# Reordering the steps of a mixer stage: each attention pair behind the states of the same quarter

## The chip, the cores and the metric

The kernel runs on one core of a Trainium2 chip. That core has five engines, each of which works through its own instruction queue in order: TensorE (PE, matrix products; its weight loads are listed as PEld), VectorE (DVE), ScalarE (ACT), GpSimd (POOL) and SyncE (SP, which here issues most of the transfers). Semaphores make one queue wait for another. The metric is the device time of one execution in microseconds (us).

## The reference

Two layers work on x, 512 positions of 1024 features, all in float32. In layer 0 one projection gives four parts of 512 features, u, q, k and v. The part u feeds a diagonal state space model of 32 groups, each with 64 complex states; q, k, v feed eight heads of stick-breaking attention. Both results go through one output projection. Layer 1 has a convolution module instead. Each mixer, and each MLP behind it, is followed by a layer norm over `alpha*x + branch(x)`.

```python
h = x @ mix_w_in[i] + mix_b_in[i]
u, q, k, v = jnp.split(h, [S5_WIDTH, S5_WIDTH + SB_WIDTH, S5_WIDTH + 2 * SB_WIDTH], axis=-1)
...
    # s5_mixer
    bu = jnp.einsum('blgp,gnp->blgn', ug, b_bar)
    _, states = lax.associative_scan(combine, (a, bu), axis=1)
    y = jnp.real(jnp.einsum('blgn,gpn->blgp', states, c)).reshape(bsz, seq, S5_WIDTH)
    y = jax.nn.gelu(y + d.astype(f32) * uf).astype(u.dtype)
    h = y @ w_glu + b_glu
    val, gate = jnp.split(h, 2, axis=-1)
    return val * jax.nn.sigmoid(gate)
...
    # stick_breaking_attention, one block of queries
    z = jnp.einsum('bqhd,bkhd->bhqk', q_blk.astype(jnp.float32), kf) * scale
    log_beta = jax.nn.log_sigmoid(z)
    log_keep = jnp.where(strict, jax.nn.log_sigmoid(-z), 0.0)
    after = lax.cumsum(log_keep, axis=3, reverse=True) - log_keep
    weights = jnp.where(strict, jnp.exp(log_beta + after), 0.0)
    return jnp.einsum('bhqk,bkhd->bqhd', weights, vf)
...
mix = jnp.concatenate([s5_out, sb_out], axis=-1) @ mix_w_out[i] + mix_b_out[i]
```

## The kernel before

Activations lie transposed, features on the partitions and the 512 positions along the free axis. To keep float32 accuracy, each large product is made of three: an operand is split into a high and a low half (`split`, lines 196 and 197; for weights lines 86 to 90, where ACT writes `whi` and DVE writes `wlo`), and `gemm` (line 206) adds high x high, high x low and low x high. One 128 x 512 output tile over eight feature tiles thus takes 24 products.

The change touches the mixer stage of layer 0, about the first 275 us. Its steps are:

- u0 to u3: four projections that give u. `u0` is spread between the transposes of x at the very start (line 298), the others come from `in_proj`. Each result is copied out of PSUM by ACT (`ue`), written to DRAM and read back in another layout as `U` (lines 592 and 594).
- the parameters of the state space model: a chain of small DVE operations (`sm`), and the output matrices `Craw`, loaded by SP and transposed by PE (`cp`, line 582) into `Cd`.
- `tables(q)`: sines and cosines for quarter q of the groups, eight scalings and three further passes on ACT and five passes on DVE, into tiles `tc` and `ts`.
- q0 to q3 (`qkv`): for one pair of heads the three projections q, k and v, 72 products. The halves of q and k (`qh`, `ql`, `kh`, `kl`) are made from PSUM by ACT and DVE.
- s0 to s3 (`s5_states`): for a quarter of the groups DVE builds the matrices `Gx` and `Cx`, PE transposes `Gx` (`gp`, line 513), multiplies (`tp` line 521, `vR` line 533, `vI` line 535), and DVE rotates by the tables, scans (lines 549 and 550) and rotates back into `Sx`.
- y0 to y3 (`s5_outputs`): twelve products (`yp`, lines 563 and 565) and the update of `U`.
- a0 to a3 (`attention`): for one pair of heads transposes of v (`vt`), scores (`z`, line 646), the softplus on ACT and DVE (`sp`), a causal select on POOL (line 638), a split (`sh`, `sl`), triangular sums added to the scores (line 670), an Exp (`w`), another select, and the product with v (`av`, line 679).
- gelu (Tanh on ACT, then through DRAM into another layout, `Yd` and `yf`), glu (products `gg` and `gv`, a Sigmoid) and at last the mixer's output product, first its half from glu (`acmo`), then its half from the attentions.

The list `ORDER` is the order in which the steps are emitted. It isn't yet the order on the engines. A planner at build time lets each engine take, among the instructions that it reckons to be ready, the one emitted first; the weight loads and splits of this stage are ranked ahead of all else. Buffers of one tag are handed out in the order of emission. PSUM has three banks under the tag `mm` (projections, `gg`, `gv`, `acmo`), four under the tag `z` (states, scores, `vt`, `yp`, `cp`) and one for `av`. The tables have three buffers each, `qh` and `ql` two each, `kh` and `kl` one each; weights are prepared up to two units ahead into three slots.

ACT holds one set of function tables at a time. `Act` (line 137 loads a set) ties each load behind all functions of the set before in the order of emission, so sets change in that order only: Sin for the tables, Exp and Ln for the attentions, Tanh for gelu, Sigmoid for glu.

Of the kernel before, what the change touches and what calls it, by code (L numbers as in the profile page):

```python
# [9 lines left out]
F32 = mybir.dt.float32  # L10
# [6 lines left out]
P = 128  # L17
T = 512
# [26 lines left out]
ATT = "sB0 sC0 wB0 sA0 wC0 sB1 sC1 wB1 sA1 wC1 wA1 wA0"  # L45
MIX_BUFS = (3, 4, 1, 4, 3)
WARM = 24
QK_BUFS = (2, 1)
ORDER = "q0 s0 q1 y0 t3 s1 a0 y1 s2 q2 y2 s3 a1 y3 gelu a2 q3 glu a3".split()


class Weights:
# [56 lines left out]
def units_of(name, w, k0, nk, cols, width):  # L109

    ncol = 1024 // nk
    out = []
    for c in cols:
        base = c // width * width
        src = w[k0 * P : (k0 + nk) * P, base : base + width].rearrange("(k p) n -> p k n", p=P)
        out.append(((name, k0, base), src, nk, ncol, c - base, width))
    return out
# [29 lines left out]
def kernel(ctx: ExitStack, tc: tile.TileContext, a: dict, out: bass.AP):  # L147
    nc = tc.nc
    act = Act(tc)
    V, S, G, PE = nc.vector, nc.scalar, nc.gpsimd, nc.tensor  # L150
# [4 lines left out]
    def const(shape, name, dt=F32):  # L155
        return cst.tile(shape, dt, tag=name, name=name)
# [5 lines left out]
    ident = const([P, P], "ident")  # L162
# [27 lines left out]
    def pv(n, i):  # L190
        if n == "mix_b_in":
            return PB[:, i : i + 1]
        return PV[:, vrow[n] + i : vrow[n] + i + 1]
# [6 lines left out]
    def gemm(ps, w, ksl, xs, c0, c1, start=True, stop=True):  # L200
        hi, lo = w
        n = len(xs)
        for k in range(n):
            xh, xl = xs[k]
            for i, (u, v) in enumerate(((hi, xh), (hi, xl), (lo, xh))):
                ins = PE.matmul(ps[:, c0:c1], u[:, k, ksl], v[:, c0:c1], start=start and k == 0 and i == 0,  # L206
                                stop=stop and k == n - 1 and i == 2).ins
        return ins
# [6 lines left out]
    s5 = mix.enter_context(tc.tile_pool(name="s5", bufs=1))  # L215

    w_in, w_glu, w_out = a["mix_w_in"][0], a["s5_w_glu"][0], a["mix_w_out"][0]
    units = units_of("u", w_in, 0, 8, range(0, 512, 128), 128)
    for o in ORDER:
        if o[0] == "q":  # L220
# [8 lines left out]
    def psum(tag, name, bufs):  # L229
        return mps.tile([P, T], F32, tag=tag, name=name, bufs=bufs)  # L230

    def mm(name):
        return psum("mm", name, MIX_BUFS[0])

    def zz(name):
        return psum("z", name, MIX_BUFS[1])
# [22 lines left out]
    xin = []  # L259
    with tc.high_priority():  # L260
        for j in range(KT):
            tag, bufs = (("spt", MIX_BUFS[3]), ("wt", MIX_BUFS[4]), ("qh", QK_BUFS[0]))[(0, 1, 0, 1, 0, 1, 0, 2)[j]]
            xt = att.tile([P, 4, P], F32, tag=tag, name=f"xin{j}", bufs=bufs)
            nc.sync.dma_start(xt, a["x"][0][:, P * j : P * (j + 1)].rearrange("(b p) f -> p b f", p=P))
            xin.append(xt)
# [3 lines left out]
    Craw = [s5.tile([P, 4, P], F32, tag="sp", name=f"Craw{i}", bufs=6) for i in range(2)]  # L269
# [22 lines left out]
    xs, w0, u0 = [], None, mm("u0")  # L292

    def u0_part(k, after):

        xh, xl = xs[k]
        for i, (u, v) in enumerate(((w0[0], xh), (w0[0], xl), (w0[1], xh))):
            ins = PE.matmul(u0, u[:, k], v, start=k == 0 and i == 0, stop=k == KT - 1 and i == 2).ins
            tc.add_manual_dep(ins, after, NOSYNC, reason="order of the first products")
            after = ins.name  # L300
        return ins

    u0_last = ready
    for j in range(KT):
        ps = (mm if j % 2 else s5ps)(f"xT{j}")
# [12 lines left out]
        if j > 1:  # L318
            u0_last = u0_part(j - 2, ins.name)
# [9 lines left out]
    for k in (KT - 2, KT - 1):  # L329
        u0_last = u0_part(k, u0_last.name)  # L330
# [10 lines left out]
    def ts(o, x, s1, s2, op0, op1):  # L341
        V.tensor_scalar(o, x, s1, s2, op0=op0, op1=op1)
        return o
# [77 lines left out]
    for k in (2, 3, 4):  # L421
        h = 1 if k < 4 else 2
# [31 lines left out]
    def spage(name, tag="sp", bufs=6):  # L454
        return s5.tile([P, 4, P], F32, tag=tag, name=name, bufs=bufs)

    tabs = []

    def tables(q):
        fa, fb, fr = spage(f"fa{q}"), spage(f"fb{q}"), spage(f"fr{q}")  # L460
        for r in range(4):
            k = 4 * q + r
            act(fa[:, r], cix, AF.Copy, scale=uh[:, k : k + 1])
            act(fb[:, r], cix, AF.Copy, scale=ul[:, k : k + 1])
        ts(fr, fa, MAGIC, MAGIC, ALU.add, ALU.subtract)
        V.tensor_tensor(fa, fa, fr, op=ALU.subtract)
        V.tensor_tensor(fa, fa, fb, op=ALU.add)
        ts(fr, fa, MAGIC, MAGIC, ALU.add, ALU.subtract)
        V.tensor_tensor(fa, fa, fr, op=ALU.subtract)
        tc_, ts_ = spage(f"tc{q}", "tabc", 3), spage(f"ts{q}", "tabs", 3)  # L470
        act(ts_, fa, AF.Sin, scale=TWOPI)
        act(fb, fa, AF.Abs)
        act(tc_, fb, AF.Sin, bias=hpi_c, scale=-TWOPI)
        tabs.append((tc_, ts_))

    for q in range(3):
        tables(q)

    Gx = s5.tile([P, 2, 4, 4, 2, 16], F32, tag="Gx", name="Gx")
# [79 lines left out]
    def s5_outputs(q):  # L559
        yp = s5ps(f"yp{q}")  # L560
        for r in range(4):
            o = yp[:, r * P : (r + 1) * P]
            PE.matmul(o, Tx[:, r], U[:, 4 * q + r], start=True, stop=False)
            for i in range(2):
                PE.matmul(o, Cx[:, i, r, 1:5].rearrange("p t g q -> p (t g q)"), Sx[:, i, r], start=False, stop=i == 1)
        for r in range(4):
            stt(U[:, 4 * q + r], U[:, 4 * q + r], DD[:, 4 * q + r : 4 * q + r + 1], yp[:, r * P : (r + 1) * P], ALU.mult, ALU.add)
        vv.append(U[:, 4 * q : 4 * q + 4])


    def in_proj(tile_i, name):
        w = W.next()
        ps = mm(name)
        gemm(ps, w, slice(0, P), xs, 0, T)
        return ps, pv("mix_b_in", tile_i)

    Cd = s5.tile([P, 2, 16, 16], F32, tag="Cd", name="Cd")
    with tc.issue_after(u0_last):
        for i in range(2):
            cp = zz(f"cp{i}")  # L580
            for b in range(4):
                PE.transpose(cp[:, b * P : (b + 1) * P], Craw[i][:, b, :], ident)
            cv = cp.rearrange("p (r g q) -> p r g q", g=2, q=16)
            for h in range(2):
                hp = slice(h * 64, h * 64 + 64)
                V.tensor_copy(Cd[hp, i], cv[hp, :, h, :])
    Ud = [tc.dram_tile([P, T], F32, name=f"Ud{j}") for j in range(4)]
    for j in range(4):
        ps, b = in_proj(j, f"u{j}") if j else (u0, pv("mix_b_in", 0))
        up = att.tile([P, T], F32, tag="wt", name=f"ue{j}", bufs=MIX_BUFS[4])  # L590
        act(up.rearrange("p (t c) -> p c t", t=4), ps.rearrange("p (c t) -> p c t", t=4), AF.Identity, bias=b)
        nc.sync.dma_start(Ud[j], up)
        for t in range(4):
            nc.sync.dma_start(U[32 * t : 32 * t + 32, 4 * j : 4 * j + 4, :],
                              Ud[j].rearrange("(r f) (t c) -> t f r c", r=4, t=4)[t])
# [6 lines left out]
    def qkv(p):  # L602
        r = []
        for s, n in enumerate("qkv"):
            ps, b = in_proj(4 + 4 * s + p, f"{n}{p}")
            if s == 2:
                t_ = att.tile([P, T], F32, tag=n, name=f"{n}{p}")
                act(t_, ps, AF.Identity, bias=b)
            else:
                b = b if s else bq8[:, p : p + 1]  # L610
                t_ = tuple(att.tile([P, T], F32R, tag=n + x, name=f"{n}{x}{p}", bufs=QK_BUFS[s]) for x in "hl")
                act(t_[0], ps, AF.Identity, bias=b)
                stt(t_[1], ps, b, t_[0].bitcast(F32), ALU.add, ALU.subtract)
            r.append(t_)
        return r
# [111 lines left out]
    hq = {}  # L727
    for o in ORDER:
        if o[0] == "q":
            hq[o[1]] = qkv(int(o[1]))  # L730
        elif o[0] == "a":
            attention(int(o[1]), *hq[o[1]])
        elif o[0] == "t":
            tables(int(o[1]))
        elif o[0] == "s":
            s5_states(int(o[1]))
        elif o[0] == "y":
            s5_outputs(int(o[1]))
        elif o == "gelu":
            gelu()  # L740
        else:
            glu()
# [31 lines left out]
    def stp(name):  # L774
        return sps_.tile([P, T], F32, tag="st", name=name)
# [181 lines left out]
    xs, first = tail_norm_lead(cat[4:8], "a", rb[0], ("ln1_g", 0), ("ln1_b", 0), LEAD, "fl0")  # L957
# [7 lines left out]
    for f in range(2):  # L965
        wn = tmp(f"wn{f}")[:CONV]
        nc.sync.dma_start(wn, a["conv_w_dw"][0][:, f * T : (f + 1) * T])
        ps = stp(f"wd{f}")
# [8 lines left out]
    xs, first = tail_norm_lead(hs, "b", rb[1], ("ln2_g", 0), ("ln2_b", 0), 4, "pl")  # L977
# [58 lines left out]
    cs_, ws, ps = None, [None] * KT, [None] * KT  # L1036
# [16 lines left out]
    for c0, c1 in HALVES:  # L1053
# [9 lines left out]
        r = ln.norm(ys, c0, c1)  # L1063
# [12 lines left out]
    xs, first = tail_norm_lead(cs_, "d", None, ("ln1_g", 8), ("ln1_b", 8), LEAD, "fl1")  # L1076
# [109 lines left out]
```

## Time and profile before

| what | value |
| --- | --- |
| median of 3 runs | 1262.05 us (1260.14 to 1264.09) |
| the profiled execution | 1257.71 us |
| its span | 1255.9 us |
| PE busy | 1203.1 us |
| DVE busy | 777.0 us |
| ACT busy | 565.1 us |
| POOL busy | 111.5 us |
| mean granted clock of PE | 0.984 |

A row of the timeline shows the start, the duration (both in us), the engine, the line, the operation and `out<-in`, then how many instructions it merges; brackets hold the idle time before it and what ended that. A name is that of the tile with buffer numbers left out, so `z1B` is a score tile of attention 1 and `q` stands for all four q projections. A row of stretches gives the length, the busy time of each engine in it with the number of instructions, then the clock that PE was granted (1.00 is full), the share of the transfer engines in use and the GB/s. Products overlap, so a product that shows 0.39 us follows the one before it after some 0.23 us. In a row of waits stand the waiting engine with its tile, who released it, the total in us, the number of waits and the longest.

### The profile page before, as it was taken

What the parts mean: (1) busy time and instruction counts of PE and PEld (TensorE: products, weight loads), DVE (VectorE), ACT (ScalarE), POOL (GpSimd) and SP (SyncE); (2) the same over time, 40 slices, a digit from 0 to 9 for tenths busy, and PEclk for the clock granted to TensorE, in tenths of its full rate; (3) what the DMA queues carried; (4) which work ended last, traced back from release to release, by engine and by line L of the source; (5) the groups of instructions that cost most, each with busy time, mean ns of one, the idle gap of its engine ahead of it and who ended that gap; (6) DMA issues with size and microseconds to landing.
All of it is one profiled execution on the core that took longest, in us unless ns stands there. A gap on an engine that the chain in (4) does not pass through costs nothing.

```text
span 1255.9 us, 16680 instructions
## 1 busy us (share of the span) xinstructions
PE 1203.1 (96%) x6559; PEld 1017.5 (81%) x6559; DVE 777.0 (62%) x1321; ACT 565.1 (45%) x1020; POOL 111.5 (9%) x145
## 2 busy tenths in 40 slices
PE   8999988999999999999999999789899999999997
PEld 6886765778988888888999889679898888888885
DVE  5996953548843433433468999999872442444446
ACT  5755465633622422323345566886462341323230
POOL 1002021103000000000031001123500000000000
PEclk8999998999999999999999999899899999999999
DMA  7520111141432333332223221004052232323211
GB/s 189 162 66 17 52 47 55 51 147 55 146 102 91 99 101 101 101 101 100 73 69 100 68 68 35 1 1 135 1 172 96 68 134 67 105 79 117 85 51 67
DMA packets 111662, 105.93 MB, mean 84 GB/s; under 512 B 9378, under 2 KB 99746, under 8 KB 111584
## 3 DMA queue, kind: packets, MB, share of 16 engines
q1 hardware_dynamic: 111424, 104.84, 26.7%
q8 instruction: 51, 0.84, 0.3%
q14 instruction: 27, 0.22, 0.1%
q10 hardware_dynamic: 160, 0.03, 0.0%
HBM read 100.66 MB, written 4.19 MB: 83 GB/s over the span
## 4 chain that ended last, share of the span: by engine, by line
PE 71%; DVE 15%; issue 6%; ACT 4%; DMA 2%; SPq 1%; POOL 1%; DVEq 0%; POOLq 0%; ACTq 0%
PE f L206 23%; PE g L1116 11%; PE acf L206 10%; PE fl L206 4%; PE h L1100 3%; PE tld L206 3%; DVE cz L350 3%; PE tlb L206 2%; PE cv L1015 2%; DVE wlo L90 2%; DVE cy L350 2%; PE av L679 2%; PE acmo L206 1%; PE pl L206 1%; PE pv L206 1%
## 5 line engine op out<-in xcount | busy, mean ns | idle before, releaser
L89 ACT CAST whi<-raw 128x1024 fp32r<-128x1024 f32 x176 | 183.8, 1049 | 409.4 <-PE f L206 111.3
L90 DVE TENSOR_TENSOR wlo<-raw,whi 128x1024 fp32r<-128x1024 f32 x176 | 219.4, 1250 | 222.9 <-ACT whi L89 222.3
L1116 PE MATMUL g<-whi,hh 128*128 128x512 f32 x208 | 81.5, 392 | 0.0
L1116 PE MATMUL g<-wlo,hh 128*128 128x512 f32 x208 | 81.5, 392 | 0.0
L1116 PE MATMUL g<-whi,hl 128*128 128x512 f32 x208 | 81.4, 391 | 0.0
L206 PE MATMUL f<-xdh,whi 128*128 128x512 f32 x208 | 80.9, 389 | 0.0
L206 PE MATMUL f<-xah,whi 128*128 128x512 f32 x208 | 80.9, 389 | 0.0
L206 PE MATMUL f<-xal,whi 128*128 128x512 f32 x208 | 80.9, 389 | 0.0
L206 PE MATMUL f<-xdh,wlo 128*128 128x512 f32 x208 | 80.9, 389 | 0.0
L206 PE MATMUL f<-xdl,whi 128*128 128x512 f32 x208 | 80.9, 389 | 0.0
L206 PE MATMUL f<-xah,wlo 128*128 128x512 f32 x208 | 80.9, 389 | 0.0
L206 PE MATMUL acf<-hl,whi 128*128 128x512 f32 x192 | 75.2, 392 | 0.0
L206 PE MATMUL acf<-hh,whi 128*128 128x512 f32 x192 | 74.9, 390 | 0.0
L206 PE MATMUL acf<-hh,wlo 128*128 128x512 f32 x192 | 74.7, 389 | 0.0
L196 ACT CAST hh<-fr 128x512 fp32r<-128x512 f32 x64 | 39.7, 621 | 71.4 <-DVE fr L346 71.3
L197 DVE TENSOR_TENSOR hl<-fr,hh 128x512 fp32r<-128x512 f32 x64 | 44.2, 691 | 37.3 <-ACT hh L196 37.2
L350 DVE SCALAR_TENSOR_TENSOR cy<-hp,wdw,cy 128x512 f32<-128x512 f32 (+1 forms) x91 | 60.8, 677 | 0.1
L350 DVE SCALAR_TENSOR_TENSOR cz<-hp,wdw,cz 128x512 f32<-128x512 f32 (+1 forms) x86 | 59.7, 698 | 0.1
L1015 PE MATMUL cv<-hph,dh 128*128 128x256 f32 (+1 forms) x113 | 39.5, 350 | 10.0 <-ACT hph L196 8.3
L346 DVE TENSOR_TENSOR fr<-fr 128x512 f32<-128x512 f32 x64 | 43.7, 684 | 5.4 <-ACT fr L135 5.4
L1116 PEld LDWEIGHTS g<-whi,hl 128*128 128x128 f32 x208 | 39.1, 188 | 8.6
L1116 PEld LDWEIGHTS g<-wlo,hh 128*128 128x128 f32 x208 | 39.1, 188 | 8.6
(684 smaller groups left out, 3182.8 us busy)
## 6 DMA issues: line engine op xcount, KB each, us to landing
raw<-in_ffn_w_dram SPq DMA_DIRECT2D x48, 1024.0 KB, 5.4
raw<-in_ffn_w_dram SPq DMA_DIRECT2D x32, 512.0 KB, 3.4
raw<-in_conv_w_pw_dram SPq DMA_DIRECT2D x12, 1024.0 KB, 5.3
raw<-in_mix_w_in_dram SPq DMA_DIRECT2D x16, 512.0 KB, 3.9
xin<-in_x_dram SPq DMA_DIRECT2D x8, 256.0 KB, 4.1
raw<-in_s_w_glu_dram SPq DMA_DIRECT2D x4, 512.0 KB
raw<-in_mix_w_out_dram SPq DMA_DIRECT2D x4, 512.0 KB
raw<-in_mix_w_out_dram SPq DMA_DIRECT2D x2, 1024.0 KB
```

What stands on the lines that cost most here:

```text
L89: i0 = nc.scalar.copy(hi, raw).ins
L90: i1 = nc.vector.tensor_sub(lo, raw, hi.bitcast(F32)).ins
L196: i0 = S.copy(hi, src).ins
L197: i1 = V.tensor_sub(lo, src, hi.bitcast(F32)).ins
L206: ins = PE.matmul(ps[:, c0:c1], u[:, k, ksl], v[:, c0:c1], start=start and k == 0 and i == 0, stop=stop and k == n - 1 and i == 2).ins
L346: V.tensor_tensor(o, x, y, op=op)
L350: V.scalar_tensor_tensor(o, x, s, y, op0=op0, op1=op1)
L679: PE.matmul(av[R, P * kb :], vt[:, kb, R], w_[:, o : o + T - P * kb], start=summed[h] == 1, stop=summed[h] == 4, skip_group_check=True)
L1015: PE.matmul(cps[j][:, c0:c1], u, v[:, t + c0 : t + c1], start=t == 0 and i == 0, stop=t == n - 1 and i == 2)
L1100: PE.matmul(ps, u, v, start=k == 0 and i == 0, stop=k == nk - 1 and i == 2)
L1116: PE.matmul(pss[b], u, v[:, kk, :], start=k + kk == 0 and i == 0, stop=k + kk == nb - 1 and i == 2)
```

## The change

The emission order becomes s, a, the next projections, y for each quarter: a0 moves from behind s1 to behind s0, a1 from behind s3 to behind s1, a2 from behind gelu to behind s2, and q3 ahead of y2 and s3. Only a3 stands behind gelu, and glu comes last. All four tables are made up front, so `tables(3)` leaves the list (`t3`), and the tables get a fourth buffer each; `qh` and `ql` lose one buffer each. The transposes of `Craw` and the copies into `Cd` are put into a function that is called behind the projection u1, where they stood behind u0. The order of the weight units stays what it was.

```diff
-QK_BUFS = (2, 1)
-ORDER = "q0 s0 q1 y0 t3 s1 a0 y1 s2 q2 y2 s3 a1 y3 gelu a2 q3 glu a3".split()
+QK_BUFS = (1, 1)
+ORDER = "q0 s0 a0 q1 y0 s1 a1 q2 y1 s2 a2 q3 y2 s3 y3 gelu a3 glu".split()
...
-        tc_, ts_ = spage(f"tc{q}", "tabc", 3), spage(f"ts{q}", "tabs", 3)
+        tc_, ts_ = spage(f"tc{q}", "tabc", 4), spage(f"ts{q}", "tabs", 4)
...
-    for q in range(3):
+    for q in range(4):
         tables(q)
...
+    proj_last = []
+    Cd = s5.tile([P, 2, 16, 16], F32, tag="Cd", name="Cd")
+
+    def c_states(last):
+        with tc.issue_after(last):
+            for i in range(2):
+                cp = zz(f"cp{i}")
+                for b in range(4):
+                    PE.transpose(cp[:, b * P : (b + 1) * P], Craw[i][:, b, :], ident)
+                cv = cp.rearrange("p (r g q) -> p r g q", g=2, q=16)
+                for h in range(2):
+                    hp = slice(h * 64, h * 64 + 64)
+                    V.tensor_copy(Cd[hp, i], cv[hp, :, h, :])
+
     def in_proj(tile_i, name):
         w = W.next()
         ps = mm(name)
-        gemm(ps, w, slice(0, P), xs, 0, T)
+        proj_last[:] = [gemm(ps, w, slice(0, P), xs, 0, T)]
         return ps, pv("mix_b_in", tile_i)
 
-    Cd = s5.tile([P, 2, 16, 16], F32, tag="Cd", name="Cd")
-    with tc.issue_after(u0_last):
...
     for j in range(4):
         ps, b = in_proj(j, f"u{j}") if j else (u0, pv("mix_b_in", 0))
+        if j == 1:
+            c_states(proj_last[0])
...
-        elif o[0] == "t":
-            tables(int(o[1]))
```

More of the change, by code (lines that the diff above doesn't have):

```diff
@@ L261 @@
         for j in range(KT):
-            tag, bufs = (("spt", MIX_BUFS[3]), ("wt", MIX_BUFS[4]), ("qh", QK_BUFS[0]))[(0, 1, 0, 1, 0, 1, 0, 2)[j]]
+            tag, bufs = (("spt", MIX_BUFS[3]), ("wt", MIX_BUFS[4]), ("qh", 1))[(0, 1, 0, 1, 0, 1, 0, 2)[j]]
             xt = att.tile([P, 4, P], F32, tag=tag, name=f"xin{j}", bufs=bufs)
@@ L573, in in_proj @@
         ps = mm(name)
-        gemm(ps, w, slice(0, P), xs, 0, T)
+        proj_last[:] = [gemm(ps, w, slice(0, P), xs, 0, T)]
         return ps, pv("mix_b_in", tile_i)
-    Cd = s5.tile([P, 2, 16, 16], F32, tag="Cd", name="Cd")
-    with tc.issue_after(u0_last):
[L579 to L586, printed above, removed]
     Ud = [tc.dram_tile([P, T], F32, name=f"Ud{j}") for j in range(4)]
```

## The prediction

> **What bounds the kernel now.** I read the page first, then the busy times by stretches cut at the steps of the mixer stage (the one stage that the change touches), then what ended the waits there.
>
> ```profile
> span 1255.9 us, 16680 instructions
> PE 1203.1 (96%) x6559; PEld 1017.5 (81%) x6559; DVE 777.0 (62%) x1321; ACT 565.1 (45%) x1020; POOL 111.5 (9%) x145
> PE 71%; DVE 15%; issue 6%; ACT 4%; DMA 2%; SPq 1%; POOL 1%; DVEq 0%; POOLq 0%; ACTq 0%
> ```
> ```profile
> core 0: us, PE busy (x) PEld busy (x) DVE busy (x) ACT busy (x) POOL busy (x), PEclk, DMA share, GB/s
> 16.40:57.20 40.80, 37.03 (x156) 30.10 (x155) 32.61 (x124) 25.30 (x52) 0.64 (x1) 0.92 0.62 161
> 57.20:81.80 24.60, 23.95 (x185) 20.45 (x184) 22.28 (x38) 12.83 (x24) 0.63 (x1) 1.00 0.30 86
> 81.80:119.70 37.90, 34.13 (x237) 25.32 (x236) 27.73 (x51) 21.74 (x43) 6.92 (x13) 1.00 0.10 29
> 119.70:139.90 20.20, 19.46 (x165) 16.28 (x164) 19.45 (x36) 5.53 (x9) 0.82 (x1) 1.00 0.16 53
> 139.90:178.80 38.90, 35.38 (x233) 26.09 (x232) 27.29 (x49) 24.10 (x47) 9.01 (x12) 0.96 0.09 28
> 178.80:221.20 42.40, 37.01 (x154) 25.22 (x153) 20.17 (x34) 27.98 (x51) 3.90 (x12) 0.92 0.22 62
> 221.20:256.90 35.70, 33.61 (x156) 23.47 (x154) 17.22 (x26) 23.45 (x41) 4.11 (x12) 1.00 0.14 45
> 256.90:274.80 17.90, 17.04 (x75) 13.80 (x75) 10.04 (x12) 5.64 (x6) 0.00 (x0) 1.00 0.49 166
> ```
>
> PE is the bound, and its work stays the same: every matrix product is still there. So the change can only move PE's losses: idle time, and clock that the throttle did not grant. In the rows of stretches, loss is length minus PE busy, plus (1 - clock) times PE busy. From 57.2 on that is 0.65 (s0, q1, k1, v1); 3.77 (s1, a0, y1); 0.74 (s2, y2); 3.52 + 1.42 = 4.94 (s3, a1, y3); 5.39 + 2.96 = 8.35 (gelu and a2, the first output gates); 2.09 (a3); 0.86 (first mixer output): 21.4 us. Before 57.2 it is 3.77 + 2.96 = 6.7 us. The whole change plays for these 28 us.
>
> **Part by part.** *The transposes of the output matrices, behind the second unit.* PE now sits before them:
>
> ```profile
> PE cp L582 <- DMA Craw<-in_s_c_im_dram: 2.1, 1, 2.1
> PE cp L582 <- DMA Craw<-in_s_c_re_dram: 1.7, 1, 1.7
> 22.00:27.00 5.00, 5.00 (x15) 3.90 (x13) 2.48 (x18) 0.00 (x0) 0.00 (x0) 0.52 0.11 25
> 29.46 1.05 ACT L89 CAST whi<-raw 128x1024 fp32r<-128x1024 f32 x1 [10.26 <-DMA raw<-in_mix_w_in_dram]
> 30.55 1.23 DVE L90 TENSOR_TENSOR wlo<-raw,whi 128x1024 fp32r<-128x1024 f32 x1 [5.73 <-ACT whi L89]
> 40.75 0.47 PE L206 MATMUL q<-x0h,whi 128*128 128x512 f32 x1
> 41.02 0.39 ACT L135 ACTIVATE fa<-cix,sm 128x128 f32<-128x128 f32 x1
> 45.35 1.18 ACT L135 ACTIVATE ue<-u,PB 128x512 f32<-128x512 f32 x1
> 36.05 0.68 DVE L467 TENSOR_TENSOR fa<-fa,fb 128x512 f32<-128x512 f32 x1
> ```
>
> Those 3.8 us of idle, and 2.4 us (5.00 x 0.48) of the throttled clock behind them, go: unit u1 can run from 16.5 to about 22, by which time the transposes' data is there, and u2 to about 29.3. But u3 is late next: its split weights are ready at 30.5 (high) and 31.8 (low), by the rows of the third load, and these do not move. So PE idles some 2 us there; u3 ends near 37, where q0 now starts at 40.75. Then q0, k0, v0 follow, and these need PSUM that ACT frees: the copy of u3 sits at 45.35, and the fourth sine and cosine table, now emitted with the other three, puts four microseconds of ACT work (8 scalings that start 0.3 us apart though each shows 0.39, and three passes of some 0.6) ahead of it, and some 2.5 us on DVE (five passes of up to 0.68) ahead of s0's matrices. Only 1.4 to 2.9 us of the lead survive to v0's end; I take 2.0. The ends: 0, if the table eats all, and 6.7, the whole loss of the stretch. The table's DVE time is hidden: q1's 24 products (5.5 us) can run while s0 waits. Its old place cost nothing either (PE lost 0.65 us in that stretch).
>
> *Attention behind the same quarter's states.* The "z" banks are handed out in program order, four in all, to states and attention alike; so one states step and the attention behind it form one serial window, filled by projections. The old order has two such windows, s1 with a0 and s3 with a1, 37.9 and 38.9 us long; the new one has four, and the first three have q1 to q3 (72 products each) as filling. Nothing new in them on PE, so each keeps a loss like the two rows: 3.77 and 4.94, mean 4.35, three times 13.05 us. Ends: 2.09 each (the row of a3, where DVE is half idle) and 4.94 plus a starved mask (below).
>
> *The last window.* Filling runs as early as it can (q3 is emitted behind a2, and now starts at 132.44, ahead of s3, a1 and a2), so q3, k3 and v3 are used up in a2's window. From s3's first transpose to the first sigmoid, PE has only s3, y3, a3 and what of the gate products fits in three PSUM banks:
>
> ```profile
> 132.44 0.48 PE L206 MATMUL q<-x0h,whi 128*128 128x512 f32 x1
> 139.87 1.04 PE L513 MATMUL gp<-ident,Gx 128*128 128x128 f32 x8
> 143.16 1.16 PE L533 MATMUL vR<-U,gt 128*128 128x128 f32 x8
> 144.16 1.06 PE L535 MATMUL vI<-U,gt 128*128 128x128 f32 x8
> 146.05 1.72 PE L521 MATMUL tp<-Cx,Gx 128*32 128x128 f32 x62
> 79.10:82.00 2.90, 2.84 (x24) 2.64 (x23) 0.00 (x0) 1.00 0.38 113
> 221.20:256.90 35.70, 18.02 (x72) 12.95 (x71) 1.00 0.14 45
> 145.84 0.69 DVE L346 TENSOR_TENSOR m<-vR,tc 128x512 f32<-128x512 f32 x1
> 154.08 1.27 DVE L346 TENSOR_TENSOR Sx<-m,n 128x508 f32<-128x508 f32 x2
> 179.46 1.03 DVE U L350 x4
> 184.05 1.28 ACT L137 ACT_TABLE_LOAD   x1
> 185.34 0.63 ACT L141 ACTIVATE sp2B<-sp2B 128x512 f32<-128x512 f32 x1
> 235.73 0.63 ACT L141 ACTIVATE sp3B<-sp3B 128x512 f32<-128x512 f32 x1
> 253.19 1.08 ACT L141 ACTIVATE w3A<-z3A 128x512 f32<-128x512 f32 x2 [2.86 <-PE z3A L670]
> 254.29 1.28 ACT L137 ACT_TABLE_LOAD   x1
> 256.94 16.79 PE acmo L206 x73
> ```
>
> Its length: 15.5 us from the transposes (139.87) to the end of the scanned states (154.08 + 1.27); 2.8 us of y3 (the row of the yp products alone); 5.9 us from U through gelu's tanh to the first Exp behind the reloaded table (179.46 to 185.34), because ACT changes tables strictly in program order and gelu now stands ahead of a3; 18.5 us of a3 from its first Exp to its last (235.73 to 254.27); 1.3 us of table load, since glu stands behind a3. Together 44.0 us. PE's work in it: s3 5.2 (1.04 + 2.06 + 2.1), y3 2.84, a3 15.6 (33.61 busy less 18.02 of L206 in that stretch), and 36 gate products at 0.23 (16.79 / 73) 8.3: 31.9. It idles 12.1 us. Ends: 1, if 11 us of projections are left for it, and 17, if only one bank's gate products fit (24 x 0.23 = 5.5 less). Behind idle time the clock falls, and I take the 1.5 us that the stretch of a1 paid:
>
> ```profile
> 160.00:168.00 8.00, 7.73 (x27) 5.10 (x27) 4.49 (x9) 3.84 (x9) 4.13 (x4) 0.79 0.21 66
> ```
>
> The Trainium skill ("TensorE: Matmul & The Clock Gate", Part 1) says that an idle window of about 3.4 us halves the clock until a window of the same length has been busy. A mean of 0.79 over 8 us is what 3.4 us at half rate gives, so the row agrees; by that rule a gap with two such windows would cost an estimated 3.4 us, and the time would be 1.9 us higher.
>
> *Smaller parts.* One buffer in place of two for q's halves: q1's copy waits in PSUM for the last score of a0, as k1's does already; two of the three projection banks are then held and one is left to run ahead, which is enough for v1; zero, with 5.5 us (one 24-product unit) as the upper end, and no gain. The weight units keep their order, so the load queue of SP loses nothing; gelu's sixteen writes and four reads through DRAM move with it, behind a2 now, and their latency lies beside a3. One table load fewer (1.28 us on an engine that is 45% busy): zero. The masks and decay selects on POOL move with their steps. What used to run under a2 (gelu's round trip, 8.35 us lost) is the part that is saved.
>
> *Sum.* New losses from s0 on: 0.65 + 13.05 + 12.1 + 1.5 + 0.86 = 28.2 us, against 21.4: 6.8 more; less 2.0 at the start: 4.8 us slower. The profiled execution took 1257.71 us, 1.8 beyond its span and 4.3 below the median of the runs shown; it would become 1262.5, and the median 1266.9.
>
> **The rivals.** *Steadier DVE (not slower).* Today DVE is 96% busy from 119.7 to 139.9, because two states steps follow each other; in the new order one states step meets one attention in every window, and masks and splits wait less. If each of the three windows lost only what a3's stretch loses (2.09), 6.8 us would go and the result is 2.0 us faster: 1260. It decides from 2.8 us a window downwards (4.8 us saved over three). For it: a3's stretch, with DVE busy 48% of the time, loses least of the three with an attention. Against: in every window the chain of rotations and scans (145.84 to 155.35, 9.5 us) stands right ahead of the attention's softplus.
>
> *The last gap is filled (faster).* The first three windows hold 23.6 + 16.6 = 40.2 us of PE work each for some 38 us of latency, so two projections (11 us) may still be waiting when s3 begins. Then the idle falls from 12.1 to 1.1, and the time is 1262.05 + 4.8 - 11 = 1255.9. It decides from 4.8 us of filling. Against: the projections of q3 are emitted ahead of y2 and s3, and run greedily today.
>
> *Starved masks (slower still).*
>
> ```profile
> 156.03 0.41 POOL L638 TENSOR_SCALAR_AFFINE_SELECT sp1B<-sp1B 128x256 f32<-128x256 f32 x1 [17.68 <-DVE sp1B L350]
> 157.55 5.68 POOL L638 TENSOR_SCALAR_AFFINE_SELECT sp1B<-sp1B 128x256 f32<-128x256 f32 x1 [0.30 <-DVE sp1B L350]
> ```
>
> The same select takes 0.41 us or 5.68 us, and the long one ends as DVE's unbroken run ends. If two more windows pay such a 5.27 us in the open, 10.5 us come on top: 1277.4. The Trainium skill ("SBUF — State Buffer", section on the two separate sides) says that certain DVE operations and POOL exclude each other for a whole instruction; that agrees with these two rows. Against: with the fillings of q1 to q3 at hand, PE need not wait for one mask.
>
> *It does not do what it says at the start:* u3's weights and the fourth table eat the 2.0 us; then 1269, inside the forecast's own range.
>
> **How the numbers follow.** Forecast, 5 us slower: 0.45, its own range 1263 to 1273. Steadier DVE 0.19, gap filled 0.15, starved masks 0.15, something else 0.06. What a measurement of this kernel can tell from no change is about 0.3%, 3.8 us. Of the forecast's share I count a quarter within that; of steadier DVE half within and a third faster; the filled gap all faster, the starved masks all slower. Slower 0.53, same 0.23, faster 0.24. The range runs from the filled gap (1255) to the starved masks with a microsecond or two more (1279).
>
> **What would show it.** Right: no PE wait on the Craw loads, a wait of about 2 us on u3's weights; a stretch of some 15 us between s3's transposes and a3's first Exp in which PE is half idle, with nothing but s3, y3 and a3's scores on it; sigmoid behind a3's last Exp; three windows of s and a with 3 to 5 us lost each. Wrong: projections between s3's products, or windows that lose 2 us; or, on the other side, selects of several microseconds in all of a0, a1 and a2.

## The result and the profile after

The changed kernel takes 1275.11 us in the median of 4 executions (1274.49 to 1277.66); the kernel before took 1261.10 us beside it. The ratio is 1.0113, with a 95% interval from 1.0087 to 1.0139: 14.0 us slower. A second measurement of the same changed kernel on another occasion (`e5` below) gave 1.0098 [1.0080, 1.0117].

The profiled execution took 1277.66 us, at the upper end of its kind, while the one shown of before lay at the lower end of its own. So I read the second profile of the changed kernel (1274.22 us) beside the first. The page of the first, its span and busy times:

```profile
span 1275.9 us, 16671 instructions
PE 1212.0 (95%) x6559; PEld 1026.5 (80%) x6559; DVE 778.6 (61%) x1321; ACT 564.8 (44%) x1019; POOL 109.5 (9%) x145
```

PE has the same 6559 products, so the 20 us of span are losses again: idle time, and clock that was not granted. The stretches of the first profile, cut at each quarter's first transpose (`gp`, here called the gate of the quarter; the gate products of glu are something else) and at the first product of the attentions' half of the output product (`tla`), which ends the block; columns as before, length, busy time of PE, PEld, DVE, ACT, POOL, granted clock:

```profile
16.40:54.80 38.40, 35.20 (x157) 27.78 (x156) 30.95 (x118) 27.89 (x59) 0.00 (x0) 1.00 0.63 167
54.80:106.50 51.70, 44.59 (x270) 33.61 (x269) 33.59 (x59) 27.91 (x51) 6.25 (x14) 0.93 0.16 45
106.50:153.70 47.20, 44.28 (x270) 33.36 (x268) 29.75 (x53) 23.09 (x44) 6.95 (x13) 0.93 0.11 34
153.70:201.10 47.40, 44.29 (x270) 33.59 (x269) 29.96 (x53) 24.36 (x45) 6.70 (x13) 0.93 0.11 34
201.10:292.80 91.70, 76.53 (x391) 59.55 (x389) 53.43 (x86) 43.29 (x70) 4.05 (x12) 0.87 0.24 76
```

The same stretches in the second profile of the same kernel:

```profile
16.40:55.80 39.40, 35.21 (x157) 27.79 (x156) 31.03 (x118) 28.00 (x59) 0.00 (x0) 1.00 0.62 163
55.80:108.40 52.60, 45.49 (x269) 34.26 (x268) 33.60 (x58) 28.01 (x51) 6.44 (x14) 0.90 0.16 44
108.40:153.20 44.80, 42.12 (x271) 31.31 (x271) 29.85 (x53) 23.10 (x44) 6.94 (x13) 1.00 0.13 36
153.20:198.00 44.80, 41.94 (x270) 31.19 (x268) 29.89 (x53) 24.36 (x45) 6.69 (x13) 1.00 0.12 36
198.00:289.40 91.40, 75.84 (x390) 58.93 (x389) 53.40 (x85) 43.33 (x70) 4.05 (x12) 0.89 0.25 76
```

The block ended at 274.8 us before; it ends at 292.8 and 289.4 us now. The two profiles differ by the two middle windows, 47.2 and 47.4 us at a clock of 0.93 or 44.8 us at 1.00; the first window and the stretch behind the last gate are alike within a microsecond. The waits of PE in the first profile (waiting tile, who released it, total us, number, longest):

```profile
PE z3B L676 <- ACT sh3B L196: 5.9, 1, 5.9
PE tp L521 <- DVE Cx L346: 4.5, 2, 3.5
PE yp L565 <- DVE Sx L346: 2.7, 1, 2.7
PE tp L521 <- DVE Cx L350: 1.7, 1, 1.7
```

No wait on the `Craw` loads is left. In its place `tp`, the products behind s0's transposes, wait for `Cx` on DVE for 5.2 us (3.5 and 1.7; the remaining 1.0 of the row lies in a later quarter), and the other two long waits, of a3's triangular sums (5.9 us) and of y3 (2.7 us), lie behind s3. Behind the block the rest of the kernel takes 983.1 us, where it took 981.1; the change does not touch it, and I did not follow these 2 us.

### The profile page after: what moved, and what is told of

Its sections match the earlier page's. It is cut to its first block, busy times and chain, and to the rows that moved or that the text cites. A ratio compares the mean times of both kernels' runs of the same rounds, so it can differ in the third digit from the quotient of the medians.

```text
span 1275.9 us, 16671 instructions
## 1 busy us (share of the span) xinstructions
PE 1212.0 (95%) x6559; PEld 1026.5 (80%) x6559; DVE 778.6 (61%) x1321; ACT 564.8 (44%) x1019; POOL 109.5 (9%) x145
## 4 chain that ended last, share of the span: by engine, by line
PE 75%; DVE 15%; ACT 3%; issue 3%; DMA 2%; POOL 1%; SPq 1%; DVEq 0%; ACTq 0%; POOLq 0%
PE f L206 22%; PE g L1120 11%; PE acf L206 10%; PE fl L206 4%; PE h L1104 3%; PE tld L206 3%; DVE cz L350 2%; PE tlb L206 2%; PE cv L1019 2%; DVE cy L350 2%; PE acmo L206 2%; DVE wlo L90 2%; PE pl L206 1%; PE pv L206 1%; PE v L206 1%
```

## The experiments

They ask three things: which part of the change costs how much, what makes s0 wait for `Cx`, and what sets the length of the stretch behind the last gate.

### One part alone

`e1`: the kernel before with the transposes of `Craw` behind u1, nothing else.

```diff
-    with tc.issue_after(u0_last):
-        for i in range(2):
...
+        if j == 1:
+            c_states(proj_last[0])
```

> The kernel before with one part of the change alone: the output matrices' transposes behind the projection u1. Theory (the start gains, the order of the steps loses): PE no longer waits 3.8 us for the Craw loads, u3 waits about 1.5 us for its weights instead, and the kernel is 2 to 4 us faster than before. Rival (the start is worth nothing, because s0 waits for Cx on DVE at the same time as before): the lead is lost ahead of s0 and the time is that of before within 1.5 us.

Measured: 1263.51 us against 1263.58, ratio 1.0005 [0.9985, 1.0024]. The first gate comes at 52.8 us where it came at 57.2, so the start does gain 4.4 us in its profile. But s0 gives it back. PE's waits between 50 and 90 us in `e1`:

```profile
PE tp L521 <- DVE Cx L350: 3.5, 1, 3.5
PE tp L521 <- DVE Cx L346: 1.5, 2, 1.0
```

And DVE's own rows in `e1`, in the order of its queue (start, duration):

```profile
56.28 1.21 DVE L90 TENSOR_TENSOR wlo<-raw,whi 128x1024 fp32r<-128x1024 f32 x1
57.41 0.74 DVE L350 SCALAR_TENSOR_TENSOR kl<-k,PB,kh 128x512 fp32r<-128x512 f32 x1
58.16 0.49 DVE L350 SCALAR_TENSOR_TENSOR Cx<-cm 64x320 f32<-64x320 f32 x1
```

The last piece of `Cx`, 0.49 us of work, stands behind a weight split and a split of k. PE goes on at 58.70 us, where the kernel before went on at 59.23, and its next 62 products, which took 1.72 us there, take 3.19 us behind the wait. An earlier gate on PE is worth nothing while DVE hands out the matrices at nearly the old time.

`e2`: the kernel before with the new order alone, the fourth table still behind y0.

```diff
-ORDER = "q0 s0 q1 y0 t3 s1 a0 y1 s2 q2 y2 s3 a1 y3 gelu a2 q3 glu a3".split()
+ORDER = "q0 s0 a0 q1 y0 t3 s1 a1 q2 y1 s2 a2 q3 y2 s3 y3 gelu a3 glu".split()
```

> The kernel before with the new order of the steps alone: tables of quarter 3 still behind y0, two buffers for the halves of q, transposes still behind u0. Theory (the order carries the loss, its last window above all): 13 to 18 us slower than before, with some 13 us of PE idle between s3's transposes and a3's last Exp. Rival (four tables up front, and the single buffer, carry it): at most 4 us slower than before.

Measured: 1270.13 us, ratio 1.0048 [1.0032, 1.0064], 6.1 us slower by its interval's middle: less than the 13 to 18 us of the theory, more than the 4 us of the rival. Two of its stretches, the last middle window and the one from the last gate to the end of a3:

```profile
150.00:194.50 44.50, 41.96 (x270) 31.17 (x269) 29.58 (x53) 24.38 (x45) 6.76 (x13) 1.00 0.11 36
194.50:247.50 53.00, 40.01 (x234) 29.98 (x232) 30.85 (x57) 29.50 (x55) 4.03 (x12) 0.81 0.19 50
```

A middle window loses only 2.5 us (44.5 less 41.96). The stretch behind the last gate loses 13.0 us of idle time, as the theory had it, and 7.6 of clock.

`e6`: the kernel before with all four tables up front and one buffer for the halves of q, old order.

```diff
-QK_BUFS = (2, 1)
+QK_BUFS = (1, 1)
...
-    for q in range(3):
+    for q in range(4):
```

> The kernel before with all four tables up front (four buffers each) and one buffer for the halves of q; order of the other steps and transposes as before. Theory (the fourth table takes DVE time ahead of s0's Cx, and q1 does not cover it because the queue has it behind tp): s0's start moves by at most 2.5 us, so 0 to 3 us slower than before. Rival (the tables make the 5 us between the changed kernel and the one with tables late): 4 to 6 us slower.

Measured: 1264.11 us against 1262.45, ratio 1.0021 [1.0007, 1.0035], 2.7 us. A small cost that is there, where the prediction had zero; which of the two edits carries it was not separated. PE's rows at s0 in `e6`, and the first product of q1 behind them (`vR` and `vI` run in between):

```profile
60.57 0.64 PE L521 MATMUL tp<-Cx,Gx 128*32 128x128 f32 x2 [2.25 <-DVE Cx L346]
62.66 3.19 PE L521 MATMUL tp<-Cx,Gx 128*32 128x128 f32 x62 [1.45 <-DVE Cx L350]
68.34 0.48 PE L206 MATMUL q<-x0h,whi 128*128 128x512 f32 x1
```

PE waits 3.7 us for `Cx`, where the kernel before waits 0.6, although q1 stands next in the list: its products stand behind s0's on PE's queue.

`e3`: the changed kernel with the fourth table back behind y0, in three buffers.

```diff
-ORDER = "q0 s0 a0 q1 y0 s1 a1 q2 y1 s2 a2 q3 y2 s3 y3 gelu a3 glu".split()
+ORDER = "q0 s0 a0 q1 y0 t3 s1 a1 q2 y1 s2 a2 q3 y2 s3 y3 gelu a3 glu".split()
...
-    for q in range(4):
+    for q in range(3):
```

> The changed kernel with the tables of quarter 3 made behind y0 again, in three buffers. Theory: the 5.2 us that PE waits for Cx of s0 shrink by the 2.5 us that the fourth table takes on DVE, so 2 to 3 us faster than the changed kernel, some 11 us slower than before. Rival (the tables up front are the main cause): within 4 us of the kernel before.

Measured: 1272.65 us, ratio 1.0068 [1.0041, 1.0094]. That lies below the whole change (1.0098 and 1.0113), with intervals that overlap: some 4 us may be the table's, in line with `e6`, but this run alone does not show it. s0 still waits 3.5 us for the last piece of `Cx`.

`e5`: the changed kernel itself, a second time.

> The changed kernel once more, beside the next three on one chip. Its two middle windows showed a granted clock of 0.93 in its profile, 47.2 and 47.4 us long; in the profiles with tables late or filling moved the same windows had a clock of 1.00 and 44.7 us. Theory (that difference is the clock's chance and not the four tables): windows of some 44.7 us in this profile, and 9 to 12 us slower than before. Rival (the early tables cost 5 us): 47 us windows again and 14 us slower than before.

Measured: 1273.92 us, ratio 1.0098 [1.0080, 1.0117]. Its middle windows of 44.8 us at full clock say that the 47 us of the first profile are not a property of the order. The parts taken alone add to 0.05 + 0.21 + 0.48 = 0.74%, the whole costs 0.98% to 1.13%: the order costs about half. The 3 to 5 us in between would be what appears only when the parts meet, but the intervals of the three parts, each some 0.15% to 0.2% to either side, are too wide together to show them.

### The tables and the wait for `Cx`

`e10`: the changed kernel with only the first table up front, the others behind s0.

```diff
-ORDER = "q0 s0 a0 q1 y0 s1 a1 q2 y1 s2 a2 q3 y2 s3 y3 gelu a3 glu".split()
+ORDER = "q0 s0 t1 t2 t3 a0 q1 y0 s1 a1 q2 y1 s2 a2 q3 y2 s3 y3 gelu a3 glu".split()
...
-    for q in range(4):
+    for q in range(1):
...
```

> The changed kernel, but only the tables of pair 0 are built up front; the other three follow s0 (7.5 us of VectorE and about 12 us of ScalarE are taken from ahead of s0's wait for Cx). Theory (s0 waits for Cx because the tables' VectorE work lies ahead of it): the wait of 5.2 us of s0's transposes for Cx falls to about 1 us, and the time is 3 to 5 us below the changed kernel. Rival (the work is owed in any case, and a0's softplus waits instead): the time stays within 2 us of the changed kernel.

Measured: 1281.45 us, ratio 1.0156 [1.0136, 1.0177], some 6 us slower still. On the cause the theory holds: the wait of s0 for `Cx` falls from 5.2 us to none in the list of PE's waits up to the second gate. On the time both expectations fail. ACT's rows in `e10`, the function set of the softplus loaded behind the last table, and the first Exp of a0:

```profile
90.95 1.28 ACT L137 ACT_TABLE_LOAD   x1
94.59 0.61 ACT L141 ACTIVATE sp0B<-sp0B 128x512 f32<-128x512 f32 x1
```

In the changed kernel this first Exp is at 68.70 us. ACT's function sets change in program order, so tables moved behind s0 hold back a0's softplus by 26 us, and its window grew from 51.7 to 64.0 us, though with 29 products more in it.

`e11`: the kernel before with the transposes moved and the tables as late as their users allow.

```diff
-ORDER = "q0 s0 q1 y0 t3 s1 a0 y1 s2 q2 y2 s3 a1 y3 gelu a2 q3 glu a3".split()
+ORDER = "q0 s0 t1 q1 t2 y0 t3 s1 a0 y1 s2 q2 y2 s3 a1 y3 gelu a2 q3 glu a3".split()
...
-    for q in range(3):
+    for q in range(1):
```

> The kernel before with the output matrices' transposes behind the second unit, and only pair 0's tables up front; the others follow s0, q1 and y0. Theory (the start's gain of the moved transposes is lost at s0's wait for Cx, which the tables hold back): with the tables out of the way the wait is below 1.5 us, and the time is 3 to 5 us below the kernel before, 1257 to 1260 us. Rival (another instruction of VectorE or ScalarE holds Cx): within 1.5 us of the kernel before.

Measured: 1260.16 us against 1261.88, ratio 0.9989 [0.9972, 1.0005]: not told apart from no change, and short of the 3 to 5 us of the theory. The wait for `Cx` is 0.3 us here. The next thing in line took its place. From the waits of PE in `e11`:

```profile
PE vR L533 <- ACT gt L515: 3.7, 1, 3.7
```

and from ACT's rows, the copies that it waits for:

```profile
58.21 1.04 ACT L89 CAST whi<-raw 128x1024 fp32r<-128x1024 f32 x1 [5.18 <-DMA raw<-in_mix_w_in_dram]
59.16 0.68 ACT L135 ACTIVATE v<-v,PB 128x512 f32<-128x512 f32 x1
59.74 1.06 ACT L515 COPY gt<-gp 128x512 f32<-128x512 f32 x2
```

ACT sat idle for 5.18 us at the head of its queue until a weight load landed, with the copies of the transposes (`gt`), whose source was complete at 54.9 us, queued behind the cast. The weights did not arrive earlier, and the lead won on PE ends there.

### The stretch behind the last gate

`e7` and `e8`: gelu's Tanh is replaced by a function that needs no change of function set, in the changed kernel and in the one before. The output of gelu is not computed in either.

```diff
-            act(g1, g1, AF.Tanh, scale=GELU_C)
+            act(g1, g1, AF.Identity, scale=GELU_C)
```

> The changed kernel with gelu's Tanh replaced by an Identity, which every table set holds: gelu is wrong then, its instructions are the same in number and size, but no set of tables is changed for it, and a3's Exp need not stand behind it. Theory (a3's softplus waiting for gelu empties the last window): a3's first Exp runs some 12 us earlier, the idle time between s3's transposes and the first sigmoid falls from 13 us to 6 or less, 6 to 12 us faster than the changed kernel. Rival (the window is bound by the chain of s3, y3 and the round trip through DRAM): only the two loads go, at most 3 us faster.

> The kernel before with the same replacement (its gelu is wrong in the same way). Theory: a2 stands behind gelu there and had v3's products as cover, so it gains less than the changed kernel, 2 to 5 us. Rival (the order of tables costs both the same): it gains as much as the changed kernel does, and the difference between the two orders stays what it is.

Measured: 1274.52 us for `e7`, ratio 1.0100 [1.0077, 1.0123], the same as the changed kernel; 1257.09 us for `e8`, 0.9969 [0.9947, 0.9992], 3.9 us less than before, within its theory's 2 to 5. In `e7` the first and the last Exp of a3:

```profile
212.09 0.62 ACT L141 ACTIVATE sp3B<-sp3B 128x512 f32<-128x512 f32 x1
249.50 0.60 ACT L141 ACTIVATE w3A<-z3A 128x512 f32<-128x512 f32 x1
```

The first moved from 226.04 to 212.09 us, the last stayed (248.99 in the changed kernel). So the theory that a3 is late because its Exp waits for gelu's function set falls; something else holds the last one at the same time. What that is no run singles out; the rows show y3's wait for `Sx` (2.6 us), and gate products ahead of a3's second half, as below.

`e12`: the changed kernel with 44 idle products, which nothing reads, where PE waits: 8 ahead of y3, 12 and 24 behind a3's scores.

```diff
+        if q == 3:
+            idle(8, vl)
...
+            if p == 3 and g in ("A0", "B1"):
+                idle(12 if g == "A0" else 24, ins)
```

> The changed kernel with 44 products more, which nothing reads: 8 ahead of y3's products, 12 behind the scores of a3's first half and 24 behind those of its second half, where TensorE is idle. Theory (idle time lowers TensorE's clock, and y3 and a3's sums then run at half their rate): the granted clock of the last window rises from 0.78 to above 0.9, and the stretch from the last gate to the last output of the block falls from 91.4 to about 87 us, the time by 4 to 5 us. Rival (the chain of ScalarE, VectorE and GpSimd behind s3 sets the stretch, and TensorE's rate only follows): the clock rises, but the stretch stays within 1.5 us of 91.4 us.

Measured: 1272.20 us, ratio 1.0083 [1.0059, 1.0107]. The stretch behind the last gate in `e12`, up to a3's end and as a whole:

```profile
198.40:250.40 52.00, 45.26 (x282) 33.67 (x281) 32.91 (x60) 30.07 (x55) 4.71 (x12) 1.00 0.22 61
198.40:287.80 89.40, 80.68 (x435) 61.90 (x433) 53.47 (x85) 43.40 (x70) 4.71 (x12) 1.00 0.26 78
```

The clock is 1.00 throughout, and the stretch is 89.4 us where it was 91.4 and 91.7. So full clock is worth 2.0 us here, between the two expectations, though by the rows the changed kernel lost 8 to 10 us of clock in it. (It is a difference of single profiles, and the idle products stand on PE's queue themselves.) y3 shows where it was gained: its products, from the first to the end of the last, take 5.2 us in the changed kernel (from 215.21) and 3.2 us in `e12` (from 212.49). The other slow products, as I read it, merely filled time in which PE would have waited.

`e4`: the changed kernel with q3 emitted behind s3, and k3 and v3 held back until s3's products are issued.

```diff
-ORDER = "q0 s0 a0 q1 y0 s1 a1 q2 y1 s2 a2 q3 y2 s3 y3 gelu a3 glu".split()
+ORDER = "q0 s0 a0 q1 y0 s1 a1 q2 y1 s2 a2 y2 s3 q3 y3 gelu a3 glu".split()
...
+            with tc.issue_after(vi_last[0]) if p == 3 and s else ExitStack():
```

> The changed kernel with q3 emitted behind s3 and its k and v products held behind s3's last state product, so that 48 products (11 us) lie in the last window. Theory (the last window lacks filling, while a2's window, 47.4 us, has some 9 us of products more than its latency hides): PE's idle time there falls from 13 us to 4 or less and the kernel is 7 to 11 us faster than the changed one. Rival (filling is only moved: a2's window opens by as much): the time stays within 3 us of the changed kernel's.

Measured: 1270.64 us, ratio 1.0060 [1.0040, 1.0080]. The window of a2 and the stretch of a3 in `e4`:

```profile
152.50:192.30 39.80, 36.15 (x222) 26.87 (x221) 26.11 (x48) 21.18 (x41) 6.67 (x13) 0.83 0.09 27
192.30:248.00 55.70, 46.20 (x282) 35.05 (x281) 34.98 (x62) 31.76 (x58) 4.71 (x12) 0.91 0.20 57
```

The 48 products that moved into the last stretch are missing one window earlier, where the clock is now 0.83. From the third gate to the first sigmoid `e4` takes 95.1 us (152.5 to 247.64), the second profile of the changed kernel 97.1 (153.2 to 250.32): 2.0 us come of it there. The whole gains more, 1.0060 against 1.0098 and 1.0113, which lies between the rival's 3 us and the theory's 7 to 11; where the rest is gained I did not find. Most of the filling is only moved: there is not enough for four windows.

`e9`: the changed kernel with the old ending, so that a2 and q3 lie between gelu and a3.

```diff
-ORDER = "q0 s0 a0 q1 y0 s1 a1 q2 y1 s2 a2 q3 y2 s3 y3 gelu a3 glu".split()
+ORDER = "q0 s0 a0 q1 y0 s1 a1 q2 y1 s2 y2 s3 y3 gelu a2 q3 glu a3".split()
```

> The changed kernel with its new beginning and middle, but the old ending: q3 is emitted behind s2 and y2, gelu and a2 lie between y3 and a3, so that a2's products stand in the stretch in which the changed kernel has only s3, y3 and a3. Theory (the last window is where the time is lost): the last output of a's block comes 8 to 12 us earlier than in the changed kernel, and the time is 1262 to 1266 us, within 3 us of the kernel before. Rival (attention behind the same quarter's states costs in each window, whatever stands at the end): the windows from gate to gate stay at 44.7 us, and the time stays within 3 us of the changed kernel, 1271 to 1276 us.

Measured: 1268.75 us, ratio 1.0052 [1.0032, 1.0072]: about half of the loss is back. It is neither the 1262 to 1266 us of the theory nor the 1271 and more of the rival. From the third gate to the end of the block `e9` takes

```profile
154.80:285.20 130.40, 117.05 (x659) 87.08 (x658) 83.35 (x138) 67.33 (x115) 9.79 (x25) 0.95 0.22 68
```

which is 5.8 us less than the 136.2 of the second profile (44.8 and 91.4). Its longest wait there, from the waits of PE, is that of glu's first products for gelu's result, which in the kernel before is 2.2 us long:

```profile
PE gg L206 <- ACT yh L135: 6.8, 1, 6.8
```

Where the rest of the loss stands is not separated: that wait is one candidate, and ahead of the third gate `e9` has the windows of the changed kernel (51.8 and 47.2 us in its profile).

## Why the prediction was right, and where its terms were off

The direction was right, and 1275 us lies inside the range of 1255 to 1279. The size was not: 4.8 us slower were forecast, 14.0 were measured. The forecast's own part of the range ended at 1273; what lies above it was added for starved masks, which did not come. That the time still lies inside is in so far luck. The sum of losses, length less PE busy plus the missing clock, by the prediction's own division (us):

| stretch | predicted | first profile | second profile |
| --- | --- | --- | --- |
| from 16.4 to the first gate | 6.7 - 2.0 = 4.7 | 3.2 | 4.2 |
| first window (s0, a0, y0 and filling) | 0.65 + 4.35 = 5.0 | 10.2 | 11.7 |
| second window | 4.35 | 6.0 | 2.7 |
| third window | 4.35 | 6.2 | 2.9 |
| from the last gate to the end of the block | 12.1 + 1.5 + 0.86 = 14.5 | 25.1 | 23.9 |

The sums are 32.9, 50.7 and 45.4. (The clock of a row is rounded, and busy time counts modelled ends: against the ends of the block, 279.6 predicted, 292.8 and 289.4 measured, the rows overstate the excess by 3 to 5 us.)

*The start.* Right in size up to the first gate: no `Craw` wait, and the gate 1.4 to 2.4 us earlier, 2.0 predicted. But the sum counted these 2.0 us as saved, and in `e1` such a lead does not show in the time. The step that failed is "The table's DVE time is hidden: q1's 24 products (5.5 us) can run while s0 waits". They cannot run there. In the changed kernel the first of them stands behind s0's products and a0's scores:

```profile
69.35 0.50 PE L206 MATMUL q<-x0h,whi 128*128 128x512 f32 x1
```

The old order does not let them run there either: in the kernel before the first of them starts at 62.68 us, behind all of s0's products, and in `e6` (rows above) PE waits with q1 next in the list. The kernel before had little to cover, 0.6 us, since its gate comes 2.4 us later. In the changed kernel PE idles 5.2 us at `Cx`, and the 62 products behind the wait take 3.06 us instead of 1.72. The first window lost 10.2 and 11.7 us instead of 5.0. With `e1`, `e6` and `e10` I take as shown that DVE's queue delivers `Cx` late and that the tables are part of it. `e2`, with the same order but the transposes, the table and q's buffers as before, waits 0.9 us there; its first window is 48.3 us long (56.9 to 105.2) and loses 7.5. So some 3 to 4 us of the excess go with those parts, the wait among them, by two profiles against one. The 2.5 us that `e2` loses above the prediction have no cause shown.

*The middle windows.* The 4.35 us each were too many where the clock held (2.7 and 2.9, and 2.5 in `e2`) and too few where it fell (6.0 and 6.2). The rival of a steadier DVE (2.09 each, and decisive from 2.8 downwards) came near in the undisturbed windows and was wrong about the sum; that DVE's steadiness is the reason, no run shows. The starved masks did not come: the longest select of a1 or a2 in the first profile is

```profile
122.76 2.16 POOL L644 TENSOR_SCALAR_AFFINE_SELECT sp1A<-sp1A 128x128 f32<-128x128 f32 x1 [0.28 <-DVE sp1A L350]
```

*The last window.* This is the step that failed most: 44.0 us from s3's transposes to the first sigmoid, measured 52.5 (201.1 to 253.64). The chain up to a3's first Exp was right, 24.9 us against 24.2, with y3 longer than its 2.8 us (5.2) and the other two terms a little shorter. The term "18.5 us of a3 from its first Exp to its last" was off: 23.5. From the end of the last Exp to the sigmoid it is 4.1 us, where I had the 1.3 us of the table load; a weight cast, which waited for gate products, stands between them. ACT's rows of the changed kernel:

```profile
226.04 0.63 ACT L141 ACTIVATE sp3B<-sp3B 128x512 f32<-128x512 f32 x1
236.39 0.38 ACT L141 ACTIVATE w3C<-z3C 128x256 f32<-128x256 f32 x1 [0.34 <-DVE yl L350]
241.39 0.38 ACT L135 ACTIVATE sp3C<-z3C 128x256 f32<-128x256 f32 x1 [4.62 <-PE z3C L652]
248.99 0.60 ACT L141 ACTIVATE w3A<-z3A 128x512 f32<-128x512 f32 x1 [0.56 <-PE av L685]
253.64 1.27 ACT L141 ACTIVATE sg<-gg,PV 128x512 f32<-128x512 f32 x2
```

From the last weights of one half to the first softplus of the next it is 5.0 us, in a3 of the kernel before 0.8:

```profile
242.34 0.38 ACT L141 ACTIVATE w3C<-z3C 128x256 f32<-128x256 f32 x1
243.15 0.38 ACT L135 ACTIVATE sp3C<-z3C 128x256 f32<-128x256 f32 x1
```

PE was not idle then. Its rows in the changed kernel, the last of sixteen gate products that run from 235.11 on, and the scores behind them:

```profile
238.78 0.39 PE L206 MATMUL gg<-yh,wlo 128*128 128x512 f32 x1
239.09 0.38 PE L652 MATMUL z3C<-qh,kh 64*128 64x256 f32 x1
239.53 1.08 PE L685 MATMUL av<-w3B,vt 128*64 128x384 f32 x4
240.97 0.38 PE L652 MATMUL z3C<-qh,kl 64*128 64x256 f32 x1
```

The bank of `z3C` is free once the Exp of 236.39 has read it, at 236.8. Its next scores start 2.3 us later, behind gate products, and between the second and the third of them stand the products with v (239.53 to 240.97). So the gate products that I had counted as filling stood ahead of the second half's scores on PE's queue, and with a queue in order a filling product delays the chain that it is to hide. The 4.2 us more than before (5.0 less 0.8) are most of what a3 is longer. This is read from the rows; no run took these products alone away. But `e9`, whose glu stands ahead of a3 as in the kernel before, has the 0.8 us again:

```profile
252.42 0.38 ACT L141 ACTIVATE w3C<-z3C 128x256 f32<-128x256 f32 x1
253.23 0.38 ACT L135 ACTIVATE sp3C<-z3C 128x256 f32<-128x256 f32 x1
```

Its a3 takes 18.8 us from the first Exp to the last, and in `e7` and `e12`, where gate products stand in between, the step takes 5.2 and 5.4 us. The clock term, 1.5 us, reads as 8 to 10 us in the rows, but `e12` prices it at 2.0: near, though its size was taken from another stretch. What was missing was waiting. In `e12` the first sigmoid comes at 248.75, 50.35 us behind the gate at 198.4. PE's own work in that window, at full clock, is an estimated 32.4 us by the row of `e2` (40.01 x 0.81). That leaves 18 us of waiting, where I had 12.1.

*The rivals.* "The last gap is filled" fell: no projections are left for the last window, and `e4`, which holds 48 products back for it, gets only part of the time back, since the window ahead then lacks them. "It does not do what it says at the start" came true in part, at s0 instead of u3.

## What to carry to other kernels

When a wait is said to be covered, look in the trace for what stands ahead of the waiting instruction on its own queue: a step that follows it there, however ready, waits with it. Filling in an in-order queue is only free until the chain that it covers wants the engine again, so price a window by its longest chain plus the filling that stands ahead of the chain's next step. And a lead won on one engine counts only as far as the first hand-over from another engine that still comes at its old time.

## What the runs showed of the hardware

The granted clock is partly chance. In the first profile of the changed kernel PE waits 1.19 us ahead of a1's product with v, and over the 8 us from 128 on the clock is 0.57:

```profile
128.22 1.18 PE L685 MATMUL av<-w1B,vt 128*64 128x384 f32 x4 [1.19 <-POOL w1B L644]
128.00:136.00 8.00, 7.78 (x23) 5.52 (x24) 4.50 (x10) 3.50 (x7) 1.02 (x3) 0.57 0.00 1
```

In the second profile the same instruction waits the same 1.19 us, behind the same shorter gaps (0.83, 0.24 and 0.23 us in the 6.5 us before it ends), and nothing happens:

```profile
130.21 1.08 PE L685 MATMUL av<-w1B,vt 128*64 128x384 f32 x4 [1.19 <-POOL w1B L644]
130.00:138.00 8.00, 7.79 (x36) 4.93 (x36) 4.88 (x11) 4.98 (x10) 1.91 (x6) 1.00 0.00 1
```

The difference is 2.4 us of a window (47.2 against 44.8), and it comes twice in the first profile (47.4 against 44.8 in the next window). The Trainium skill ("TensorE: Matmul & The Clock Gate", Part 1) says that the windows in which the activity of the array is counted run freely, so that the moment of a change varies from run to run; with that the two profiles agree. It also gives an idle window of about 3.4 us as what lowers the clock, and there the first profile differs: the clock fell although no gap ahead of it was longer than 1.19 us. Whether that gap did it, or the four together with the small products between them, no run here shows.

The other surprise is that a clock loss in a row is no price. The rows of the last stretch show 8 to 10 us of it, and in `e12` the same stretch at full clock was 2.0 us shorter.
